# The norms' factors with tokens on the partitions: one-column sums, a power on GpSimd, a diagonal matmul

## The chip, the core and the metric

The kernel runs on one core of a Trainium2 chip. The core has TensorE (PE, matmuls; PEld is its loading of weights), VectorE (DVE), ScalarE (ACT), GpSimd (POOL) and SyncE (SP, which issues the DMAs). Each engine works through its own queue in order and waits on semaphores for the others. The metric is the device time of one execution in microseconds (us); lower is better.

## The reference, cut to what matters

A trunk of two layers over 512 tokens with 1024 features, all float32. Each layer is a half-step SwiGLU FFN, a mixer and another half-step FFN; the first layer's mixer is RWKV-7 beside an RG-LRU, the second's is stick-breaking attention. Every one of the six sub-layers has a norm ahead of it and one behind it:

```python
def rmsnorm(x, g):
    xf = x.astype(jnp.float32)
    y = xf * lax.rsqrt(jnp.mean(xf * xf, axis=-1, keepdims=True) + NORM_EPS)
    return (y * g.astype(jnp.float32)).astype(x.dtype)
...
    x = x + FFN_HALF * rmsnorm(swiglu(rmsnorm(x, ffn1_pre_g), ffn1_w_in, ffn1_w_out), ffn1_post_g)
    x = x + rmsnorm(mixer(rmsnorm(x, mix_pre_g)), mix_post_g)
    x = x + FFN_HALF * rmsnorm(swiglu(rmsnorm(x, ffn2_pre_g), ffn2_w_in, ffn2_w_out), ffn2_post_g)
```

RWKV-7 also has a group norm over each head's 64 features, `(y - mean) * lax.rsqrt(var + GN_EPS)`.

## The kernel before

Features lie on the partitions and tokens along the row: x is eight tiles of 128 features x 512 tokens. A weight comes by DMA in chunks of 128x1024 (`wraw`) and is split into a rounded part (`whi`, ScalarE) and the rest (`wlo`, VectorE); the activations are split in the same way, and each product is three matmuls (`mm3`). A sub-layer has *units* (products with the normed input) and *out tiles* (products that give its output y). Around a border between two sub-layers the work runs in halves of 256 tokens, so that the last out tiles of one half cover the norm of the other half and the first units of the next sub-layer.

A norm's factor is 1/sqrt(mean + eps) per token. The squares of the eight tiles (ScalarE) are added into one tile `acc` (GpSimd, `sumsq`); then `rsqrt` sums over the partitions. Before the change it multiplies with a matrix of ones, which leaves the sum of each token on all 128 partitions (128x256 for a half), takes the root of all of it on ScalarE and the reciprocal of all of it on VectorE. `pre` does so ahead of a sub-layer: the factor goes to `rstd`, and the units' products are multiplied with it when they leave their bank of PSUM; the tiles hi and lo of x*g that the units read don't need it. `post` does so behind a sub-layer: y * g * factor on VectorE, added to x on GpSimd (`add`), from which hi (ScalarE) and lo (VectorE, `low`) of the next sub-layer follow. That makes 23 calls of `rsqrt`, one for each half of each norm but the very last, which `last` does through `rsqrt_bank`: there the sum has tokens on the partitions already. `unit_v` of the attention takes the same factor for v with tokens on the partitions (128x4), and `chain` of RWKV-7 the group norms' factors (128x8, four times).

The order of the work is not written out. Every piece is a thread (a generator), and `Run` merges their steps by a rough clock of the engines: a step goes out when its engine would be free by the planner's costs (`cost`), by priority among equals. Behind that stands the scheduler of the tile framework, to which `emit` gives the count of the instruction as its priority, shifted for some threads by `OFFS` (`norm`, the thread of a norm ahead of a sub-layer, comes 100 later). So a change of a step's engine or cost may move other work too. A tile stands on one of 8 banks of PSUM; units may hold six of them in an FFN (`LIMIT`), three in the mixers.

All of a thread's instructions are recorded through one line of `emit`, L366 in the profile, so groups are told apart by tiles: `ones` is the matrix of ones, `eps` the added constant, `b` any tile of the arena in SBUF.

## Time and profile before

| | us |
|---|---|
| median of 3 runs | 2136.75 |
| lowest, highest | 2135.71, 2138.49 |
| the profiled execution: its span, from the first to the last instruction | 2139.7 |
| PE busy | 2060.2 |
| VectorE busy | 1229.3 |
| ScalarE busy | 863.9 |
| GpSimd busy | 488.5 |

The profile has the profiled execution's time as its span alone. Busy time is the union of an engine's instructions; matmuls are pipelined, so a PE that is busy need not be at its peak. A row of a timeline gives start, duration, engine, line, operation, output <- input, shape and count; in brackets stands how long the engine had nothing to do before it, and whose result ended that.

### The profile page before, as it was taken

How to read it: one execution, taken by the hardware profiler on the slowest of the kernel's cores; microseconds unless marked ns; L12 is line 12 of the kernel's file. 1: busy time of each engine (PE TensorE's matmuls, PEld its weight loads, DVE VectorE, ACT ScalarE, POOL GpSimd, SP SyncE). 2: the span in 40 equal slices, each digit the busy share in tenths (PEclk: the TensorE clock that was granted, in tenths of full speed). 3: DMA queues.
4: the chain of work that ended last, by engine and by line, in shares of the span. 5: the costliest groups of instructions: out<-in, count | busy, mean ns of one | idle time of the engine just before them, and what ended most of it. 6: DMA issues, size and time to landing. Idle time of an engine off the chain costs nothing. (4 is left out here: it accounts for less than half of the span.)

```text
span 2139.7 us, 29740 instructions
## 1 busy us (share of the span) xinstructions
PE 2060.2 (96%) x11916; PEld 1747.1 (82%) x11916; DVE 1229.3 (57%) x1770; ACT 863.9 (40%) x1370; POOL 488.5 (23%) x480
## 2 busy tenths in 40 slices
PE   8999999899999899999999999999999899999998
PEld 7888889877677887888898888888878789788887
DVE  6344344887786853444466354446899977344443
ACT  6322223555655443222335322233666755322221
POOL 3000013512331620100153010015232354010013
PEclk9999999999999999999999999999999999999999
DMA  5322321322113223223312322231111223333311
GB/s 195 120 93 99 101 96 51 117 58 62 35 52 104 84 82 116 88 99 108 99 60 81 117 92 98 96 99 36 54 56 60 79 80 108 99 98 99 108 51 40
DMA packets 72378, 185.54 MB, mean 87 GB/s; under 512 B 19632, under 2 KB 26928, under 8 KB 72240
## 3 DMA queue, kind: packets, MB, share of 16 engines
q1 hardware_dynamic: 72240, 183.65, 26.7%
q8 instruction: 93, 1.52, 0.3%
q14 instruction: 45, 0.37, 0.1%
HBM read 177.85 MB, written 5.77 MB: 86 GB/s over the span
## 5 line engine op out<-in xcount | busy, mean ns | idle before, releaser
L366 PE MATMUL bank<-b,b 128*128 128x512 f32 (+6 forms) x7350 | 1232.1, 330 | 28.4 <-DVE b L366 19.5
L366 PEld LDWEIGHTS bank<-b,b 128*128 128x128 f32 (+3 forms) x7350 | 1031.6, 181 | 217.8 <-DVE b L366 36.5
L366 PE MATMUL bank<-b,whi 128*128 128x512 f32 (+1 forms) x2460 | 692.4, 365 | 20.5 <-DVE b L366 10.9
L366 POOL TENSOR_TENSOR b<-b,b 128x256 f32<-128x256 f32 (+5 forms) x355 | 364.3, 1039 | 870.7 <-DVE b L366 560.6
L366 DVE TENSOR_TENSOR b<-bank,b 128x512 f32<-128x512 f32 (+7 forms) x441 | 250.6, 582 | 527.7 <-PE bank L366 520.9
L366 PEld LDWEIGHTS bank<-b,whi 128*128 128x128 f32 x2460 | 441.8, 192 | 92.6 <-DVE b L366 14.3
L366 PE MATMUL bank<-b,wlo 128*128 128x512 f32 (+1 forms) x1230 | 447.7, 364 | 0.8 <-DVE wlo L366 0.8
L366 DVE TENSOR_TENSOR b<-wraw,b 128x1024 fp32r<-128x1024 f32 (+1 forms) x194 | 267.9, 1386 | 148.7 <-ACT b L366 130.4
L366 ACT CAST b<-wraw 128x1024 fp32r<-128x1024 f32 (+1 forms) x194 | 196.6, 1024 | 333.7 <-PE bank L366 192.4
L366 PEld LDWEIGHTS bank<-b,wlo 128*128 128x128 f32 x1230 | 235.9, 192 | 34.9 <-issue 1.2
L366 POOL TENSOR_TENSOR b<-b 128x512 f32<-128x512 f32 (+5 forms) x93 | 105.5, 1144 | 683.2 <-DVE b L366 553.3
L366 ACT ACTIVATE b<-b 128x256 f32<-128x256 f32 (+1 forms) x319 | 154.3, 501 | 243.1 <-DVE b L366 204.9
L366 ACT CAST whi<-wraw 128x1024 fp32r<-128x1024 f32 (+2 forms) x143 | 144.9, 1018 | 238.5 <-PE bank L366 170.8
L366 DVE TENSOR_TENSOR wlo<-wraw,whi 128x1024 fp32r<-128x1024 f32 (+2 forms) x143 | 201.3, 1412 | 68.0 <-ACT whi L366 67.4
L366 ACT CAST b<-b 128x512 fp32r<-128x512 f32 (+3 forms) x188 | 104.8, 560 | 220.1 <-POOL b L366 185.6
L366 DVE TENSOR_TENSOR b<-b,b 128x512 fp32r<-128x512 f32 (+12 forms) x234 | 138.2, 599 | 73.5 <-ACT b L366 72.1
L366 DVE SCALAR_TENSOR_TENSOR b<-b,par,b 128x256 fp32r<-128x256 f32 (+5 forms) x209 | 151.8, 780 | 2.5 <-ACT b L366 2.2
L366 DVE TENSOR_TENSOR_SCAN b<-b,b 128x512 f32<-128x512 f32 (+1 forms) x72 | 71.5, 1019 | 7.2 <-ACT b L366 6.8
L366 ACT COPY b<-bank 128x512 f32<-128x512 f32 (+3 forms) x104 | 50.6, 500 | 61.4 <-PE bank L366 54.9
L366 ACT ACTIVATE b<-b,par 128x256 fp32r<-128x256 f32 (+1 forms) x100 | 51.2, 520 | 54.2 <-POOL b L366 47.5
L366 ACT ACT_TABLE_LOAD x49 | 62.9, 1283 | 9.5 <-PE bank L366 8.0
L366 DVE RECIPROCAL b<-b 128x256 f32<-128x256 f32 (+3 forms) x34 | 42.3, 1243 | 22.0 <-ACT b L366 21.9
(52 smaller groups left out, 623.3 us busy)
## 6 DMA issues: line engine op xcount, KB each, us to landing
wraw<-in_w_dram SPq DMA_DIRECT2D x302, 512.0 KB
wraw<-in_w_dram SPq DMA_DIRECT2D x32, 384.0 KB
b<-in_x_dram SPq DMA_DIRECT2D x16, 128.0 KB
l_mix_residual<-b SPq DMA_DIRECT2D x8, 256.0 KB
b<-l_mix_residual SPq DMA_DIRECT2D x8, 256.0 KB
out_dram<-b SPq DMA_DIRECT2D x16, 128.0 KB
rwkv_scores<-b SPq DMA_DIRECT2D x16, 64.0 KB
b<-in_aux_dram SPq DMA_DIRECT2D x2, 256.0 KB
```

Of the source, the lines that this page charges most:

```text
L366: f(*a, **k)
```

## The change

`rsqrt` now calls `rsqrt_bank`, and that no longer needs an extra tile. The sum is made per block of 128 tokens with the squares as weights and one column of ones as the moving operand, so that the tokens lie on the partitions: 128x2 for a half. A new `root` scales it and adds eps (VectorE, out of the bank), and raises it to -0.5 (GpSimd, `pow` with a constant tile `power`). VectorE multiplies the identity with each column, which gives a diagonal matrix per block; ones times this matrix spreads the factor over the partitions, in the same bank; ScalarE copies it out. `unit_v` and the group norms use `root` as well, in place of the root on ScalarE and the reciprocal. `eps` goes. The instructions are now called through a table of lambdas by the thread's name, which only gives each thread a line of its own in the profile; comments are taken out.

```diff
-        self.eps = self.cp.tile([P, 2], F32, name="eps")
-        nc.vector.memset(self.eps[:, 0:1], EPS)
-        nc.vector.memset(self.eps[:, 1:2], GN_EPS)
+        self.power = self.cp.tile([P, 8], F32, name="power")
+        nc.vector.memset(self.power, -0.5)
...
     def rsqrt(self, acc, s, out):
-        n = s.stop - s.start
-        ps = yield from self.bank()
-        self.PE.matmul(ps[:, :n], self.ones, acc[:, s], start=True, stop=True)
-        yield
-        std = yield from self.regs(n)
-        self.S.activation(std.ap, ps[:, :n], AF.Sqrt, bias=self.eps[:, 0:1], scale=1.0 / D)
+        ps = yield from self.rsqrt_bank(acc, s)
+        self.S.copy(out, ps[:, T - (s.stop - s.start) :])
         self.drop(ps)
         yield
-        self.V.reciprocal(out, std.ap)
-        self.put(std)
-        yield
-
-    def rsqrt_bank(self, acc, s, extra):
-        """the same, tokens on the partitions for the root, left in a bank"""
+
+    def root(self, out, mean, scale, eps):
+
+        self.V.tensor_scalar(out, mean, scale, eps, op0=ALU.mult, op1=ALU.add)
+        yield
+        self.G.tensor_tensor(out, out, self.power[:, : out.shape[1]], op=ALU.pow)
+        yield
+
+    def rsqrt_bank(self, acc, s, extra=None):
+
         n = s.stop - s.start
         nb = n // P
         ps = yield from self.bank()
         for b in range(nb):
-            for i, a in enumerate((acc[:, s], extra.ap)):
-                self.PE.matmul(ps[:, b : b + 1], a[:, b * P : (b + 1) * P], self.ones[:, 0:1], start=i == 0, stop=i == 1)
-        yield
-        self.put(extra)
+            parts = (acc[:, s],) if extra is None else (acc[:, s], extra.ap)
+            for i, a in enumerate(parts):
+                self.PE.matmul(ps[:, b : b + 1], a[:, b * P : (b + 1) * P], self.ones[:, 0:1], start=i == 0,
+                               stop=i == len(parts) - 1)
+        yield
+        if extra is not None:
+            self.put(extra)
         std, diag = yield from self.regs(64, n)
         c = std[:, 0:nb]
-        self.S.activation(c, ps[:, 0:nb], AF.Sqrt, bias=self.eps[:, 0:1], scale=1.0 / D)
-        yield
-        self.V.reciprocal(c, c)
-        yield
+        yield from self.root(c, ps[:, 0:nb], 1.0 / D, EPS)
         for b in range(nb):
             self.V.tensor_scalar_mul(diag[:, b * P : (b + 1) * P], self.ident, c[:, b : b + 1])
         yield
...
         V.tensor_reduce(v, c8(sq), axis=AX.X, op=ALU.add)
         yield
-        S.activation(v, v, AF.Sqrt, scale=1.0 / 64, bias=net.eps[:, 1:2])
-        yield
-        V.reciprocal(v, v)
+        yield from net.root(v, v, 1.0 / 64, GN_EPS)
...
             rc = self.rc[:, 0:4]
-            net.S.activation(rc, ps[:, 0:4], AF.Sqrt, bias=net.eps[:, 0:1], scale=1.0 / D)
+            yield from net.root(rc, ps[:, 0:4], 1.0 / D, EPS)
             net.drop(ps)
-            net.V.reciprocal(rc, rc)
```

How the order of instructions moves, at two places. In the names a number tells one tile of a pool from another (bank_85 is a tile on a bank of PSUM, b_5 holds `acc`, par the parameters with the identity); L310 is the thread `finish` (norms behind a sub-layer), L285 `norm` (norms ahead of one), L309 the main thread, L276 and L274 the evacuations.

The first place is the border from the first layer's second FFN to the second layer's first FFN, the second half's norm behind the sub-layer. PE before, the sum among the next FFN's first units:

```order
L366 MATMUL bank_87<-b_90_6053,b_81_5554 128x256
L366 MATMUL bank_87<-b_52_2434,b_25_323 128x256
L366 MATMUL bank_85<-b_5_95,ones 128x256
L366 MATMUL bank_87<-b_52_2434,b_81_5554 128x256
L366 MATMUL bank_87<-b_90_6053,b_81_5554 128x256
```

PE after:

```order
L309 MATMUL bank_84<-b_52_2433,b_83_5578 128x256
L310 MATMUL bank_85<-ones,b_5_94 128x1 x2
L309 MATMUL bank_84<-b_100_6214,b_84_5579 128x256
L309 MATMUL bank_84<-b_85_5661,b_83_5578 128x256
L309 MATMUL bank_84<-b_111_7957,b_83_5578 128x256
L309 MATMUL bank_84<-b_85_5661,b_84_5579 128x256
L309 MATMUL bank_84<-b_85_5661,b_83_5578 128x256
L309 MATMUL bank_84<-b_111_7957,b_83_5578 128x256
L309 MATMUL bank_84<-b_85_5661,b_84_5579 128x256
L309 MATMUL bank_84<-b_39_690,b_83_5578 128x256
L310 MATMUL bank_85<-b_107_7403,ones 128x256
L309 MATMUL bank_84<-b_112_7958,b_83_5578 128x256
```

Where one matmul with ones stood, two one-column sums stand now, and the spread comes eight passes of the units later.

VectorE at the same place before, with the last weight split and evacuation ahead of the norm:

```order
L366 TENSOR_TENSOR b_101_6255<-bank_89,b_101_6255 128x256
L366 TENSOR_TENSOR b_82_5555<-wraw_76,b_91_6073 128x1024
L366 TENSOR_TENSOR b_21_221<-wraw_74,b_82_5555 128x1024
L366 RECIPROCAL b_101_6255<-b_101_6255 128x256
L366 SCALAR_TENSOR_TENSOR b_108_7870<-b_99_6226,par,b_101_6255 128x256
```

VectorE after:

```order
L276 TENSOR_TENSOR b_103_6306<-bank_88,b_103_6306 128x256
L280 TENSOR_TENSOR b_24_327<-wraw_73,b_84_5579 128x1024
L310 TENSOR_SCALAR b_107_7403<-bank_85 128x2
L310 TENSOR_SCALAR b_107_7403<-par,b_107_7403 128x128 x2
L310 SCALAR_TENSOR_TENSOR b_107_7403<-b_102_6305,par,b_107_7403 128x256
```

The reciprocal has become the affine step and the two diagonal products, which stand next to each other; between them lies GpSimd's power.

The second place is the start of the attention, the first half's norm ahead of it, on PE. Before, with the sum between the units' first products of the second half:

```order
L366 MATMUL bank_85<-b_127_10323,b_21_221 128x256
L366 MATMUL bank_84<-b_119_9695,whi_79 128x256
L366 MATMUL bank_84<-b_127_10323,whi_79 128x256
L366 MATMUL bank_86<-b_5_95,ones 128x256
L366 MATMUL bank_84<-b_119_9695,wlo_80 128x256
```

After:

```order
L309 MATMUL bank_87<-b_132_10387,b_24_327 128x256
L285 MATMUL bank_82<-ones,b_5_94 128x1 x2
L309 MATMUL bank_83<-ones,b_5_94 128x1 x2
L285 MATMUL bank_82<-b_70_4174,ones 128x256
L309 MATMUL bank_89<-b_97_6153,whi_76 128x256
```

Sum and spread stand ahead of the second half's units, with only the first two sums of `unit_v` between them.

## Rows read from the trace of the kernel before

**Rows 1.** The page's head: span, then each engine's busy us, share, instructions.

```profile
span 2139.7 us, 29740 instructions
...
PE 2060.2 (96%) x11916; PEld 1747.1 (82%) x11916; DVE 1229.3 (57%) x1770; ACT 863.9 (40%) x1370; POOL 488.5 (23%) x480
```

**Rows 2.** PE's timeline: start us, us, instruction, count [idle before <-releaser].

```profile
373.43 7.00 PE L366 MATMUL bank<-b,b 128*128 128x256 f32 x57
399.18 0.58 PE L366 MATMUL bank<-b,b 128*128 128x256 f32 x1 [3.37 <-DVE b L366]
...
713.60 1.22 PE L366 MATMUL bank<-b,ones 128*128 128x256 f32 x2 [4.21 <-POOL b L366]
...
756.02 0.80 PE L366 MATMUL bank<-b,whi 128*128 128x256 f32 x2 [3.36 <-DVE b L366]
...
1115.99 1.22 PE L366 MATMUL bank<-b,ones 128*128 128x256 f32 x2 [3.99 <-POOL b L366]
...
1494.34 0.39 PE L366 MATMUL bank<-b,whi 128*128 128x256 f32 x1 [3.03 <-DVE b L366]
...
1801.82 4.38 PE L366 MATMUL bank<-b,b 128*128 128x512 f32 x18 [1.02 <-ACT b L366]
```

**Rows 3.** Groups of one shape: count | busy us, mean ns | idle before, releasers.

```profile
L366 ACT ACT_TABLE_LOAD x49 | 62.9, 1283 | 9.5 <-PE bank L366 8.0 <-PEq L2016 0.7
L366 DVE RECIPROCAL b<-b 128x256 f32<-128x256 f32 x23 | 40.2, 1748 | 17.0 <-ACT b L366 16.9
L366 DVE TENSOR_SCALAR b<-bank 128x8 f32<-128x8 f32 x4 | 0.7, 162 | 1.4 <-PE bank L366 1.4
L366 POOL TENSOR_TENSOR b<-b,b 128x127 f32<-128x127 f32 x7 | 4.5, 640 | 5.4 <-ACT b L366 3.7 <-DVE b L366 1.7
L366 POOL TENSOR_TENSOR b<-b,b 128x512 f32<-128x512 f32 x76 | 110.3, 1454 | 632.2 <-DVE b L366 493.0 <-ACT b L366 137.1 <-DMA wraw<-in_w_dram 1.2
L366 ACT COPY b<-bank 128x256 f32<-128x256 f32 x24 | 8.1, 372 | 20.3 <-PE bank L366 19.1 <-POOL b L366 1.2
```

**Rows 4.** Timelines of PE, VectorE, ScalarE at three norms behind sub-layers.

```profile
387.80 0.59 PE L366 MATMUL bank<-b,ones 128*128 128x256 f32 x2
392.14 10.23 DVE L366 SCALAR_TENSOR_TENSOR b<-b,par,b 128x256 f32<-128x256 f32 x16
...
731.32 1.05 PE L366 MATMUL bank<-b,ones 128*128 128x256 f32 x2
737.53 0.47 ACT L366 ACTIVATE b<-bank,eps 128x256 f32<-128x256 f32 x1 [4.18 <-POOL b L366]
739.89 12.21 DVE L366 SCALAR_TENSOR_TENSOR b<-b,par,b 128x256 f32<-128x256 f32 x16
...
1484.26 0.70 PE L366 MATMUL bank<-b,ones 128*128 128x256 f32 x2 [0.67 <-POOL b L366]
1487.29 5.26 DVE L366 SCALAR_TENSOR_TENSOR b<-b,par,b 128x256 f32<-128x256 f32 x7
```

**Rows 5.** Timeline of one-column sums: the factor for v, and the last norm.

```profile
1509.64 0.50 PE L366 MATMUL bank<-ones,b 128*128 128x1 f32 x4
...
2128.26 0.83 PE L366 MATMUL bank<-ones,b 128*128 128x1 f32 x6 [0.91 <-ACT b L366]
2129.19 0.26 ACT L366 ACTIVATE b<-bank,eps 128x2 f32<-128x2 f32 x1 [0.98 <-PE bank L366]
...
2129.68 0.48 DVE L366 TENSOR_SCALAR b<-par,b 128x128 f32<-128x128 f32 x2
...
2130.31 1.19 PE L366 MATMUL bank<-b,ones 128*128 128x256 f32 x2 [1.22 <-DVE b L366]
```

**Rows 6.** GpSimd's timeline ahead of the wait at 1115.99.

```profile
1104.55 11.39 POOL L366 TENSOR_TENSOR b<-b,b 128x256 f32<-128x256 f32 x9 [0.58 <-ACT b L366]
```

**Rows 7.** ScalarE's timeline ahead of the wait at 1801.82.

```profile
1800.00 1.28 ACT L366 ACT_TABLE_LOAD   x1
1801.29 0.47 ACT L366 ACTIVATE b<-bank,eps 128x256 f32<-128x256 f32 x1
```

43 lines of the change are left out of this document (42 added, 1 removed).

## The prediction

> **What bounds the kernel now.** I read the page's head first [rows 1]: TensorE (PE) is busy 2060 of 2139.7 us, so all that can be won without touching its matmuls is some 80 us of its idle time, and anything that makes PE issue more has to be hidden in those 80 us. ScalarE, VectorE and GpSimd are busy 40, 57 and 23% of the span; they matter only where PE waits for them. So I next took PE's own timeline and looked for rows with a bracket, its waits [rows 2]. The long ones beside the norms stand at the borders of the six sub-layers: 3.37 us at 399.18 (first FFN to first mixer), 4.21 at 713.60 and 3.36 at 756.02 (mixer to FFN), 3.99 at 1115.99 (FFN to FFN), 3.03 at 1494.34 (FFN to attention), 1.02 at 1801.82 (attention to FFN). Between the borders, inside an FFN, PE does not wait. The reader is to see who releases these waits: VectorE or GpSimd five times, ScalarE once. The rest of the idle time lies in the two mixers, at the first loads and behind the last matmul, where a norm has little part.
>
> **What the change takes away.** 23 norms (12 ahead of sub-layers, 11 behind) lose a 128x256 square root on ScalarE and a 128x256 reciprocal on VectorE of 1.75 us [rows 3]; four group norms and the one root for v lose small ones. Of the 49 table loads [rows 3] the order of instructions after has 29 left: 20 x 1.28 = 25.7 us of ScalarE. What these cost on a path is read from three norms behind sub-layers, from the sum's first pass on PE to VectorE's first product with the factor [rows 4]: 387.80 to 392.14 = 4.34 us, 731.32 to 739.89 = 8.57, 1484.26 to 1487.29 = 3.03.
>
> **What it adds on PE.** The sum with 256 columns was two passes; now two blocks of one column each, in two passes, make four, and the spreading matmul with 128x256 is again two passes. So PE issues four passes more per norm. Four one-column passes took 0.50 us [rows 5], so 0.5 x 23 = 11.5 us. They cannot be free: PE is full on both sides of most norms.
>
> **What it adds as a wait.** The sum and the spread are now two visits to PE, and between them lie VectorE, GpSimd, VectorE. PE works its queue in order, so when it comes to the spread too early, all that stands behind it, the next units' products, waits too. The last norm of the kernel before already has this form, with a root on ScalarE [rows 5]: the last one-column pass ends at 2128.26 + 0.83 = 2129.09, ScalarE starts 0.10 later, the two diagonal products take 0.48 and the spread starts 0.15 after them. For the new chain I put 0.10 + 0.16 (affine of 8 columns from a bank [rows 3]) + 0.10 (hop) + P + 0.10 (hop) + 0.48 + 0.15 = 1.09 + P, where P is GpSimd's power of two columns. No row has a power. GpSimd's nearest rows are 0.64 us for 128x127 and 1.45 us for 128x512 [rows 3]; a line through both gives about 0.4 for two columns, the power itself may cost more than a product. I take P = 0.7, near the narrowest row, and keep 0.4 to 1.45. So 1.8 us, bounds 1.5 and 2.5.
>
> What covers it are the passes that the order puts between the two visits. A pass takes (7.00 - 0.28) / 56 = 0.12 us [rows 2]. Counting them in the order for the 23 norms gives 0.48 us once (the first norm of attention), 0.96 three times, 1.3 to 1.8 eleven times, and 2.2 to 6.5 for the rest. Adding up what is missing to the chain gives 5.5 us at 1.8, 2.9 at 1.5 and 16.8 at 2.5. While the power runs VectorE stands too: in 21 of 24 norms the diagonal products are the very next thing in its queue, so what is queued there (weight splits, the products with the factor, evacuations) waits 0.1 + P + 0.1 = 0.9 us. VectorE's work per norm goes from 1.75 to 0.16 + 0.48 = 0.64, so 0.2 us is what it keeps of the 1.1 it saved. GpSimd gets 0.7 us more per norm; the power stands right behind the last addition to the sum or among the residual additions.
>
> The Trainium skill (SBUF — State Buffer, "SBUF: two separate sides") says that VectorE instructions with two inputs in SBUF and GpSimd instructions that read SBUF exclude each other on a shared port. The trace agrees as far as it goes: nine additions took 11.39 us, 1.27 each, while VectorE split weights [rows 6], against 0.64 for the narrower row. By that rule a power would wait for a running VectorE instruction; but VectorE mostly stands waiting for the power, and only where something lies between would the sum grow, by my estimate of under 3 us in all.
>
> **How much of PE's cost is hidden.** Norm by norm, by the waits of [rows 2]: at 399.18 the wait follows the second half's norm behind the sub-layer, which is hidden. At 756.02 it follows that norm and the first norm ahead, two hidden. At 1115.99 GpSimd sets the end, having run without a break from 1104.55 to 1115.94 [rows 6], so the first half's norm behind the sub-layer is hidden. At 1494.34 two more. That makes 6; the other 17 stand before a chain's start or behind the last wait of their border. So 17 x 0.5 = 8.5 us and 5.5 x 17 / 23 = 4.1 us of stalls fall on the path.
>
> **What the chains give back.** From the sum to the first product with the factor the new way takes 0.6 (four passes and their end) + 1.8 + 0.6 (spread) + 0.5 (ScalarE's copy of 0.37 [rows 3] with its hops) = 3.5 us. Against 4.34 that is 0.8 us won at 399.18. Against 8.57, up to the whole wait of 3.36 at 756.02; the long part there is the root, which ScalarE started only at 737.53, with GpSimd named as what it waited for [rows 4]. The new way has no root on ScalarE, but it visits GpSimd and ScalarE as well, so the gain could also be nothing; I take 3.4. Against 3.03 it loses 0.5 at 1494.34. At 1801.82 PE waits 1.02 us for a weight's cast on ScalarE, which had a table load of 1.28 and a root in its queue from 1800.00 on [rows 7]; that goes: 1.0. At the very end 2129.09 to 2129.68 = 0.59 becomes 0.10 + 0.16 + 0.10 + 0.7 + 0.10 = 1.16, so 0.6 more. Other relief from 25.7 us less on ScalarE is between nothing and 5 us (five waits like the one at 1801.82); I take 2.5.
>
> The Trainium skill (ScalarE: Activation LUTs, "What ACT_TABLE_LOAD costs") counts a drain of 1.38 us to each load, 2.66 in all. The trace does not: the load at 1800.00 ends at 1801.28 and the root starts at 1801.29 [rows 7]. By the page the relief would be about twice as large and the sum 2.5 us lower.
>
> **The sum.** +8.5 + 4.1 - 0.8 - 3.4 + 0.5 - 1.0 + 0.6 - 2.5 = +6.0 us. The profile gives its execution by the span alone, 2139.7 us, 2.9 above the median of 2136.75; I carry the difference over to the median: 2142.8.
>
> **Rivals.** (a) *Hidden or balanced.* PE's added passes are swallowed by waits that exist, because a border's end is set by GpSimd's additions (as at 1115.99, and they are not made shorter). With half as many norms on the path (6.3 instead of 12.6) the sum is -0.3: 2136.5. For it: GpSimd and VectorE release five of six waits. Against it: PE has no wait after the second norm ahead at most borders.
> (b) *Faster.* The other side. The place is PE's two waits for GpSimd, 4.21 at 713.60 and 3.99 at 1115.99, where the planner put the sum's matmul ahead of its operand. The planner books the new steps with other lengths, and if at both places the sum comes late enough, 8.2 us go; the stalls on the path shrink with P near 0.4 by 2.6 x 17 / 23 = 1.9; and the two passes of the sum behind each of these waits took 1.22 us against 0.59 at 387.80 [rows 2, 4], 0.6 each. That gives 6.0 - 8.2 - 1.9 - 1.2 = -5.3: 2131.4. It decides from the point where the sum's first pass comes after GpSimd's last addition. Against it: at 1115.99 the order after puts the sum 166 rows behind the one before it, 163 before, so PE comes there no later.
> (c) *The power is long.* At P = 1.45 the stalls on the path are 16.8 x 17 / 23 = 12.4 instead of 4.1, the chains take 0.75 more at three places, 2.2, and give back nothing at 756.02: 6.0 + 8.3 + 2.2 + 3.4 = +19.9: 2156.7.
> (d) *The order itself.* The planner is greedy, and the mixers' instructions come in another order after as well. Nothing in the profile prices this; it is why the range reaches 4 us beyond the sums at the lower end.
>
> **How the numbers follow.** My forecast is +6.0, 2142.8; its own range from P and the shares is 2138 to 2149. About 0.2% (4.3 us) is what a measurement of this kernel can tell from no change. Chances: forecast 0.43, of which 0.08 ends within 0.2%; (a) 0.22, all within; (b) 0.27; (c) 0.08. So faster 0.27, same 0.08 + 0.22 = 0.30, slower 0.35 + 0.08 = 0.43. The range: (b) less the 4 us of (d), rounded, to (c): 2128 to 2157.
>
> **What would show it.** Right: 29 table loads; PE's instructions up by 4 passes in each of 23 norms; PE rows of the spread with waits of 0.2 to 1.5 us released by VectorE; powers of 0.4 to 1.0 us; waits at the borders about as long as before. Wrong: powers over 1.5 us; the waits at 713.60 and 1115.99 gone; spreads without waits; or a difference that lies inside a mixer, away from all norms.

## The result, and the profile after

The changed kernel takes 2205.75 us (median of 4 runs), the kernel before 2137.62 us beside it: a ratio of 1.0313, 95% interval 1.0297 to 1.033. It is slower by 68 us where 6 were forecast, and far outside the range.

The page's head after, its answer to [rows 1], and the granted clock in 40 slices:

```profile
span 2204.2 us, 29945 instructions
...
PE 2099.5 (95%) x12008; PEld 1776.7 (81%) x12008; DVE 1202.1 (55%) x1815; ACT 833.0 (38%) x1344; POOL 507.2 (23%) x509
...
PEclk9999999998998899999999999999999999999999
```

PE has 92 passes more, which is 4 for each of 23 norms, as counted. But it is busy 39 us more, not 11.5. Some of its passes must run slower, and the eights in the clock's line, in slices 10, 13 and 14 (about 496 to 551 and 661 to 772 us), say where: in the first mixer and just behind it. It is so in every run: over the whole the granted clock is 0.970 to 0.972 in the four runs of the changed kernel, and 0.982 to 0.987 in the runs of the kernel before that were timed beside the experiments.

**Where the 64.5 us of span arise.** I cut both executions at the norms' sums, which have a tile of their own (`ones`). A border runs from the first pass of the first half's sum behind a sub-layer to the first pass of the second half's sum ahead of the next; a sub-layer from there to its own first sum. For mixer 0 these are the two rows here, first of the kernel before (its end is the wait at 713.60 in [rows 2]), then of the changed one (start us, us, instruction, count):

```profile
413.75 0.59 PE L366 MATMUL bank<-b,ones 128*128 128x256 f32 x2
```

```profile
427.70 0.50 PE L285 MATMUL bank<-ones,b 128*128 128x1 f32 x4
...
757.98 1.01 PE L310 MATMUL bank<-ones,b 128*128 128x1 f32 x4 [4.04 <-POOL b L277]
```

So mixer 0 took 713.60 - 413.75 = 299.9 us before and 757.98 - 427.70 = 330.3 after. All stages in the same way: start to the first border +3.2, border into mixer 0 +10.8, **mixer 0 +30.4**, the other four borders +13.8, the three later FFNs +6.3, mixer 1 -1.1, the end +1.1. That is 64.5. Nearly half of the loss lies in a stage whose changed instructions are four group norms and, at its start, the end of the norm that opens it (the spread at 430.65).

**What happens in mixer 0.** A stage's length is PE's idle time, plus its busy time times the granted clock (work at full clock), plus the rest of its busy time (what the lower clock costs). Mixer 0 before: 12.9 idle + 278.3 work + 8.6 lower clock. After: 26.4 + 273.5 + 30.4. So the work did not grow beyond what such a split can tell (the clock has two digits, which is 1.5 us each); 13.5 us are idleness and some 20 us lower clock. The last 100 us of the mixer show both. Busy time of all engines of the changed kernel (columns: stretch, its length, busy us of PE, PEld, DVE, ACT, POOL with counts, granted clock, DMA share, GB/s):

```profile
660.00:680.00 20.00, 19.73 (x177) 14.40 (x177) 18.86 (x39) 12.47 (x22) 3.39 (x3) 1.00 0.36 100
680.00:700.00 20.00, 8.52 (x136) 7.58 (x134) 14.13 (x17) 14.30 (x18) 10.11 (x7) 0.66 0.39 125
700.00:720.00 20.00, 20.00 (x172) 14.12 (x172) 2.10 (x5) 2.80 (x7) 0.53 (x1) 1.00 0.04 14
720.00:740.00 20.00, 14.76 (x140) 12.37 (x140) 6.50 (x15) 2.61 (x6) 3.72 (x3) 0.74 0.30 93
```

The same stretches, counting only instructions that touch the rounded weights `whi`, the large products of the units and out tiles (PE, PEld, DVE, ACT, then the clock):

```profile
680.00:700.00 20.00, 0.15 (x1) 0.16 (x1) 0.00 (x0) 0.00 (x0) 0.66 0.39 125
700.00:720.00 20.00, 7.92 (x24) 4.12 (x24) 0.00 (x0) 0.00 (x0) 1.00 0.04 14
720.00:740.00 20.00, 0.00 (x0) 0.00 (x0) 0.00 (x0) 0.00 (x0) 0.74 0.30 93
```

Two rows of PE's timeline after, the longest wait of the first of these stretches, and in the last one large products whose weights are no `whi` (out tiles of a half, 128x256):

```profile
687.74 2.06 PE L291 MATMUL bank<-b,b 64*64 64x64 f32 x32 [4.21 <-DVE b L280]
...
733.60 3.94 PE L309 MATMUL bank<-b,b 128*128 128x256 f32 x31
```

And in the kernel before, 47 us earlier, about equally far from the mixer's end:

```profile
633.00:653.00 20.00, 6.64 (x18) 3.22 (x18) 1.21 (x1) 2.09 (x2) 1.00 0.20 58
653.00:673.00 20.00, 7.96 (x24) 4.35 (x24) 1.21 (x1) 0.00 (x0) 1.00 0.33 106
673.00:693.00 20.00, 6.46 (x19) 3.38 (x18) 0.00 (x0) 0.00 (x0) 1.00 0.46 145
```

The mixer has two kinds of work for PE: the recurrence of four pairs of heads, chains of small matmuls that wait for VectorE and ScalarE at every step, and the large products, which wait for little and fill what the chains leave open. Before, 5 to 8 us of products with `whi` stand in every 20 us from 593 to 693. After, they come in lumps. From 680 to 700 one of them is left: PE runs the small products of a pair almost alone (L291 is the thread `inverse`), idles 11.5 us, and its clock falls to 0.66. From 720 to 740 there is none, and the 37 half-row products stand together from 733.60 on, behind 13 us of the pair's chain alone. That the lumps cause the loss is read from such stretches; no run moves the large products by themselves. The clock falls without idleness too. In 5 us pieces of the changed kernel around 530 us:

```profile
520.00:525.00 5.00, 5.00 (x32) 4.14 (x31) 4.42 (x15) 3.22 (x5) 0.53 (x1) 1.00 0.29 105
525.00:530.00 5.00, 5.00 (x48) 3.69 (x48) 4.45 (x14) 2.63 (x4) 1.20 (x1) 0.78 0.00 0
530.00:535.00 5.00, 5.00 (x28) 3.60 (x27) 0.00 (x0) 0.11 (x1) 0.07 (x1) 0.50 0.10 26
535.00:540.00 5.00, 5.00 (x28) 3.74 (x28) 1.36 (x4) 1.36 (x3) 0.00 (x0) 0.50 0.01 3
```

From 525 to 535 no pass touches a `whi`: PE issues only the pairs' products with 64 or 128 columns, is busy without a gap, and its clock falls to half (1.2 in place of 2.4 GHz), in which it stays until some time after 545; large products return from 535 on.

**What happens at the norms.** PE's waits by line over the whole span, after (L310 is the thread of the norms behind sub-layers, L285 of those ahead; total, times, longest):

```profile
PE bank L310 <- DVE b L310: 11.5, 5, 3.8
PE bank L285 <- DVE b L285: 11.2, 6, 4.7
...
PE bank L309 <- DVE b L284: 6.9, 14, 1.8
...
PE bank L310 <- POOL b L276: 5.3, 3, 3.0
PE bank L310 <- POOL b L277: 4.5, 2, 4.0
```

The first two are the waits at the spread: 22.7 us, of which 1.62 are the last norm's, where PE waited 1.22 before too [rows 5]; in the 23 changed halves it is 21.1. Waits for GpSimd at the sums stayed, 4.04 us at 757.98 for the 4.21 at 713.60 and 2.96 at 1160.32 for the 3.99 at 1115.99 [rows 2]. The last norm shows the chain with all engines free (PE, VectorE, GpSimd):

```profile
2192.39 0.83 PE L310 MATMUL bank<-ones,b 128*128 128x1 f32 x6 [0.91 <-ACT b L276]
2193.33 0.16 DVE L310 TENSOR_SCALAR b<-bank 128x2 f32<-128x2 f32 x1 [1.50 <-PE bank L310]
2193.57 0.71 POOL L310 TENSOR_TENSOR b<-b,power 128x2 f32<-128x2 f32 x1 [3.30 <-DVE b L310]
2194.31 0.48 DVE L310 TENSOR_SCALAR b<-par,b 128x128 f32<-128x128 f32 x2 [0.82 <-POOL b L310]
...
2194.84 1.22 PE L310 MATMUL bank<-b,ones 128*128 128x256 f32 x2 [1.62 <-DVE b L310]
```

1.62 us from the end of the sum to the spread. The second half's norm at the border into mixer 0 is the same work with VectorE's queue in the way (VectorE's row ahead of it first, from its own timeline):

```profile
394.52 0.69 DVE L298 TENSOR_TENSOR b<-b,b 128x512 fp32r<-128x512 f32 x1 [1.80 <-ACT b L298]
...
391.15 0.61 PE L310 MATMUL bank<-ones,b 128*128 128x1 f32 x4 [1.62 <-POOL b L276]
395.13 0.15 DVE L310 TENSOR_SCALAR b<-bank 128x2 f32<-128x2 f32 x1
395.36 0.71 POOL L310 TENSOR_TENSOR b<-b,power 128x2 f32<-128x2 f32 x1 [4.26 <-DVE b L310]
396.10 0.48 DVE L310 TENSOR_SCALAR b<-par,b 128x128 f32<-128x128 f32 x2 [0.82 <-POOL b L310]
...
396.64 1.22 PE L310 MATMUL bank<-b,ones 128*128 128x256 f32 x2 [3.83 <-DVE b L310]
```

The sum ends at 391.76, but the affine of two columns starts at 395.13: VectorE stood behind a split of the mixer's own weights (L298) that waited for ScalarE. From the sum's end to the affine it is 0.03 to 0.33 us in 14 of the 24 norms, 1.0 to 4.3 us in the other 10, 26 us in all.

These waits are not all new idle time. PE is idle 2139.7 - 2060.2 = 79.5 us before and 2204.2 - 2099.5 = 104.7 after; without the mixer's 12.9 and 26.4 that is 66.6 and 78.3, 11.7 us more. The waits at sums and spreads grew by 20.9 us (14.8 in all before, 35.7 after). The difference is in waits that went: 3.37 us at 399.18, 3.36 at 756.02 and 3.03 at 1494.34 [rows 2] were waits for VectorE behind the norms, at other products. After, no wait in the borders is longer than 1.93 us but those at sums and spreads: PE stands at the spread in place of a later product.

### The profile page after: what moved, and what is told of

It reads as the page before. It is cut to its first block, busy times and chain, and to the rows that moved or that the text cites. A ratio compares the mean times of both kernels' runs of the same rounds, so it can differ in the third digit from the quotient of the medians.

```text
span 2204.2 us, 29945 instructions
## 1 busy us (share of the span) xinstructions
PE 2099.5 (95%) x12008; PEld 1776.7 (81%) x12008; DVE 1202.1 (55%) x1815; ACT 833.0 (38%) x1344; POOL 507.2 (23%) x509
## 4 chain that ended last, share of the span: by engine, by line
PE 75%; DVE 11%; POOL 4%; ACT 3%; issue 2%; DMA 1%; DVEq 0%; POOLq 0%; SPq 0%; ACTq 0%
PE bank L309 67%; DVE b L302 3%; PE bank L291 2%; PE bank L292 2%; DVE b L310 2%; POOL b L285 2%; DVE b L284 1%; PE bank L302 1%; DVE b L274 1%; PE bank L290 1%; DVE b L280 1%; DVE wlo L280 1%; DMA wraw<-in_w_dram 1%; PE bank L310 1%; POOL b L292 1%
## 5 line engine op out<-in xcount | busy, mean ns | idle before, releaser
L309 PE MATMUL bank<-b,b 128*128 128x512 f32 (+1 forms) x5437 | 1065.7, 354 | 10.6 <-DVE b L284 5.7
L309 PEld LDWEIGHTS bank<-b,b 128*128 128x128 f32 x5437 | 901.2, 191 | 152.1 <-DVE b L284 8.5
L309 PE MATMUL bank<-b,whi 128*128 128x512 f32 (+1 forms) x2444 | 696.0, 368 | 13.3 <-ACT b L283 8.2
L309 PEld LDWEIGHTS bank<-b,whi 128*128 128x128 f32 x2444 | 443.4, 194 | 85.8 <-ACT b L283 8.9
L309 PE MATMUL bank<-b,wlo 128*128 128x512 f32 (+1 forms) x1222 | 448.4, 367 | 0.8 <-DVE wlo L280 0.8
L274 DVE TENSOR_TENSOR b<-bank,b 128x512 f32<-128x512 f32 (+1 forms) x237 | 143.3, 618 | 320.1 <-PE bank L309 311.5
L309 PEld LDWEIGHTS bank<-b,wlo 128*128 128x128 f32 x1222 | 236.7, 194 | 35.6 <-issue 1.5
L274 POOL TENSOR_TENSOR b<-b 128x512 f32<-128x512 f32 (+1 forms) x58 | 66.9, 1156 | 582.7 <-DVE b L274 493.3
L274 POOL TENSOR_TENSOR b<-b,b 128x512 f32<-128x512 f32 (+1 forms) x42 | 54.4, 1295 | 481.9 <-DVE b L274 441.3
L274 ACT CAST b<-b 128x512 fp32r<-128x512 f32 (+3 forms) x160 | 88.6, 556 | 200.8 <-POOL b L274 181.1
L276 DVE TENSOR_TENSOR b<-bank,b 128x256 f32<-128x256 f32 (+1 forms) x88 | 47.6, 543 | 173.9 <-PE bank L309 173.9
L274 DVE TENSOR_TENSOR b<-b,b 128x512 fp32r<-128x512 f32 (+3 forms) x140 | 91.5, 654 | 62.6 <-ACT b L274 61.6
L274 ACT ACTIVATE b<-b 128x512 f32<-128x512 f32 (+1 forms) x100 | 57.1, 576 | 99.1 <-DVE b L274 98.9
L285 POOL TENSOR_TENSOR b<-b,b 128x256 f32<-128x256 f32 x84 | 83.0, 988 | 36.4 <-ACT b L285 32.5
L287 POOL TENSOR_TENSOR b<-b,b 128x256 f32<-128x256 f32 x88 | 76.7, 901 | 23.8 <-DVE b L310 23.4
L310 DVE SCALAR_TENSOR_TENSOR b<-b,par,b 128x256 f32<-128x256 f32 x87 | 65.3, 810 | 11.5 <-ACT b L310 9.7
L276 POOL TENSOR_TENSOR b<-b,b 128x256 f32<-128x256 f32 (+1 forms) x51 | 44.8, 879 | 95.8 <-ACT b L276 95.1
L284 DVE SCALAR_TENSOR_TENSOR b<-b,par,b 128x256 fp32r<-128x256 f32 x96 | 63.8, 711 | 2.3 <-ACT b L283 2.2
```

The lines of the kernel that those rows point to most:

```text
L274: "unit_ev": lambda f, a, k: f(*a, **k),
L276: "third_ev": lambda f, a, k: f(*a, **k),
L284: "low": lambda f, a, k: f(*a, **k),
L285: "norm": lambda f, a, k: f(*a, **k),
L287: "add": lambda f, a, k: f(*a, **k),
L309: "main": lambda f, a, k: f(*a, **k),
```

## The experiments

Two questions: is mixer 0's loss the power (in the group norms, or through the late border ahead), or the order that the planner made of the instructions? And what do the norms themselves cost? `LAG[1]` is a number of the planner: how many planned us the thread that ends a sub-layer's second half holds back. "Plan" is the length of mixer 0 by the planner's own rough clock, which the expectations quote. In the table it runs from the first pair's first matmul to the first sum behind the mixer. The first four expectations count the border ahead as part of the mixer, in the plan and on the chip (there 350.9 us before, 392.1 changed). Figures of a stage come from one profiled execution each, and with a clock of two digits the split of a mixer's length is good to 1.5 us; the length itself was 9 us apart in two executions of one order (the last experiment). Since the cut follows PE's order, it can also move work between a border and the stage behind it. Outside is the span less mixer 0, against the 1839.8 us of before.

| kernel | ratio to before [95%] | plan of mixer 0 | mixer 0, us | idle + lower clock there | outside, us |
|---|---|---|---|---|---|
| before | 1 | 269.8 | 299.9 | 12.9 + 8.6 | 0 |
| changed | 1.0313 [1.0297, 1.033] | 293.9 | 330.3 | 26.4 + 30.4 | +34.1 |
| norm_old | 1.0011 [0.9995, 1.0027] | 268.9 | 303.0 | 18.3 + 8.5 | +0.1 |
| b_lag4 | 1.0128 [1.0101, 1.0154] | 305.6 | 336.6 | 27.8 + 27.8 | -4.4 |
| b_lag0 | 1.0084 [1.0066, 1.0103] | 270.3 | 304.4 | 12.8 + 11.7 | +12.0 |
| a_lag2 | 1.0224 [1.0193, 1.0256] | 263.9 | 308.9 | 16.0 + 11.7 | +36.1 |
| late2 | 1.0168 [1.013, 1.0205] | 271.8 | 306.4 | 16.1 + 8.7 | +23.2 |
| cost_real | 1.0239 [1.0207, 1.0271] | 278.3 | 323.2 | 15.9 + 21.5 | +25.1 |
| gn_old | 1.0321 [1.0292, 1.035] | 304.9 | 335.3 | 26.7 + 27.8 | +31.9 |
| pre_new | 1.0283 [1.0263, 1.0302] | 294.4 | 337.8 | 27.2 + 24.8 | +23.6 |
| post_new | 1.0178 [1.016, 1.0196] | 257.9 | 313.0 | 10.2 + 24.2 | +24.2 |
| mult_for_pow | 1.0257 [1.0236, 1.0277] | 293.9 | 322.3 | 22.7 + 24.0 | +31.7 |
| gn_mult | 1.0278 [1.0256, 1.03] | 293.9 | 325.3 | 23.7 + 24.1 | +35.4 |
| norm_old_lag1 | 1.0143 [1.0117, 1.0168] | 273.9 | 320.0 | 19.8 + 15.0 | +5.2 |
| lag1_gn_mult | 1.0111 [1.0088, 1.0133] | 273.9 | 328.7 | 16.7 + 31.2 | +4.7 |

### norm_old: the two-half norms undone

```diff
     def rsqrt(self, acc, s, out):
-        ps = yield from self.rsqrt_bank(acc, s)
-        self.S.copy(out, ps[:, T - (s.stop - s.start) :])
+        n = s.stop - s.start
+        ps = yield from self.bank()
+        self.PE.matmul(ps[:, :n], self.ones, acc[:, s], start=True, stop=True)
...
+        self.V.reciprocal(out, std.ap)
```

> The changed kernel with the 22 two-half norms (pre and post) of the old form again: 128x128 sum, root on ScalarE, reciprocal on VectorE. The group norms of the RWKV mixer, the factor for v and the last norm stay with the power on GpSimd. Theory A (the order of instructions in mixer 0 is what costs some 30 us; the power itself is cheap there): the planner's own length for mixer 0, from the first sum of the post norm ahead of it to the first sum of its own post norm, is 316.2 us for this kernel, against 317.0 for the kernel before and 338.0 for the changed one, so mixer 0 should take on the chip the 350.9 us of before within 6 us, not the 392.1 of after, and the whole kernel 2130 to 2142 us. Theory B (the power of the group norms, queued on GpSimd, delays the mixer): mixer 0 stays 25 us or more over before, the whole kernel at 2160 to 2175 us.

Measured: 2145.67 us against 2143.64, no difference (both a little above the range of theory A), mixer 0 at 303.0, with the border ahead 354.0, within 6 of 350.9 as theory A had it. The power in the group norms, in v's factor and in the last norm costs nothing that can be measured in this order. So the whole loss hangs on the norms ahead of and behind the sub-layers, though nearly half of it appears in a stage that has none inside but the end of one.

### b_lag4: the old instructions, another order

```diff
-LAG = (0.0, 3.0, 0.0)
+LAG = (0.0, 4.0, 0.0)
```

> Every instruction of the kernel before (no norm is touched), with the same number of the planner moved the other way: the lag ahead of the second half's post norm is 4 us in place of 3. Its own length for mixer 0 is then 354.7 us, against 317.0 for the kernel before. Theory A (order): mixer 0 takes 380 to 410 us on the chip in place of 350.9, with none of the changed norms in it, and the whole kernel 2165 to 2200 us. Theory B (the power and the norms' new form cost the mixer its time): a lag of one microsecond at five places moves the whole by no more than 6 us, 2132 to 2143 us.

Measured: 2169.36 us, mixer 0 at 336.6, +36.7, without one changed norm. (The expectation counts the border ahead as part of the mixer: 336.6 + 54.2 = 390.8, inside its 380 to 410.) It has the same signature as the changed kernel, +14.9 us idle and +19.2 lower clock, and the same stretch, 80 us from the mixer's end:

```profile
673.00:693.00 20.00, 10.36 (x65) 6.93 (x64) 16.42 (x19) 16.66 (x23) 10.00 (x7) 0.79 0.52 151
```

An order alone is enough for the whole of mixer 0's loss.

### a_lag2 and cost_real: the changed instructions, other orders

The first sets `LAG[1]` to 2. The second tells the planner what the power takes:

```diff
+        if k.get("op") == ALU.pow:
+            return 0.39 + 0.157 * n, 0.15
         return 0.1 + (1.1e-3 if op in self.FAST else 2.25e-3) * n, 0.15
```

> Every instruction of the changed kernel, but one number of the planner is moved: the lag ahead of the second half's post norm is 2 us in place of 3. The planner then writes mixer 0 out in another order; its own length for the mixer is 306.0 us (338.0 for the changed kernel, 317.0 for the kernel before). Theory A (order): mixer 0 takes on the chip 340 to 355 us, against 392.1 in the changed kernel, and the whole kernel comes to 2150 to 2175 us; what is left over the kernel before is the borders' share of some 20 to 25 us, since the chain with the spread is unchanged there. Theory B (the power itself): mixer 0 stays at 380 us or more and the whole at 2195 to 2210 us.

> The changed kernel, with the planner told what the power takes: 0.39 us and 0.157 us for each column (0.71 us for two columns, 1.02 for four, 1.65 for eight), where it reckoned 0.10 to 0.12 us. The instructions are those of the changed kernel; the spread stands later in TensorE's queue and mixer 0 comes in another order (the planner's own length 323.3 us, 338.0 for the changed kernel). Theory A: mixer 0 at 350 to 370 us. For the borders: if the waits of TensorE at the spreads come from a power that is longer than planned, they go from 22.7 us to under 10 us and the borders give back 10 us or more, the whole at 2140 to 2165 us; if the waits come from VectorE and ScalarE being late at the borders whatever the power takes, they stay at 18 us or more and the whole is 2160 to 2180 us. Theory B (the power holds GpSimd up in mixer 0): the mixer stays over 380 us and the whole over 2185 us.

Measured, a_lag2: 2188.79 us. Counted from its own start the mixer falls from 330.3 to 308.9, with every power in place; with the border it is 367.1, because the border stayed 7.2 us long and the mixer 9 over before. That lies between the 340 to 355 of theory A and the 380 of theory B, and so does the whole. What lies outside mixer 0 did not gain (+36.1). An order that changes no instruction gives back 21 us of the mixer, less than theory A's plan said.

Measured, cost_real: 2191.67 us, above what theory A allowed and in theory B's range. The mixer fell by 7 only, though its plan was 15 shorter; with the border it is 379.8, 10 over theory A's range and next to theory B's 380. By its own expectation this run speaks for theory B; gn_old and gn_mult below decide against it. The waits at the spreads went from 22.7 to 11.8 us (7.0 and 4.8 in the two threads), and what lies outside mixer 0 from +34.1 to +25.1: 9 us for 11 us of waits. In the borders themselves nothing shows, 284.9 us for 285.4; the gain is in the FFNs behind them, 955.5 for 964.2, as it would be if PE did their first units where it had waited. PE's idle time outside the mixer fell by 5.4 us (78.3 to 72.9), not by 11: the waits for VectorE at the next sub-layer's operands (L284) rose from 6.9 to 12.8.

### gn_old: the group norms undone

```diff
...
-        yield from net.root(v, v, 1.0 / 64, GN_EPS)
+        S.activation(v, v, AF.Sqrt, scale=1.0 / 64, bias=net.eps[:, 1:2])
+        yield
+        V.reciprocal(v, v)
```

> The changed kernel with only the group norms of the RWKV mixer undone: the root on ScalarE and the reciprocal on VectorE again, no power in mixer 0's own chains. The planner's own length for mixer 0, from the first pair's first matmul to the first sum of the post norm, is 304.9 us for it, against 293.9 for the changed kernel and 269.8 for the kernel before. On the chip, mixer 0 from the last sum of the pre norm to the first sum of its post norm took 330.3 us in the changed kernel and 299.9 in the kernel before. Theory A (order): undoing this part makes the mixer no faster but as slow or slower, 328 to 348 us, the whole kernel 2200 to 2225 us. Theory B (the power on GpSimd holds the mixer up): mixer 0 returns to 300 to 310 us and the whole to 2175 to 2185 us.

Measured: 2209.14 us, mixer 0 at 335.3, 5 us more than with the power, less than two executions of one order can differ by (9 us, the last experiment). Taking the power out of the mixer's own chains does not help. Theory B, that the power on GpSimd holds the mixer up, falls.

### pre_new and post_new: one kind of norm at a time

```diff
# pre_new, in post:
-        yield from self.rsqrt(self.acc, s, rs.ap)
+        yield from self.rsqrt_old(self.acc, s, rs.ap)
# post_new, in pre:
-            yield from self.rsqrt(self.acc, s, self.rstd[:, s])
+            yield from self.rsqrt_old(self.acc, s, self.rstd[:, s])
```

> The changed kernel with the post norms of the old form and the pre norms, the group norms, v's factor and the last norm of the new one. Planner's own length of mixer 0: 294.4 us (before 269.8, changed 293.9). Theory A (order for the mixer, the new form of the norms for the borders): mixer 0 at 322 to 338 us; the five borders together, from the first half's post sum to the second half's pre sum, lie 8 to 16 us over the 260.8 us of before, where the changed kernel has 285.4; the whole 2175 to 2200 us. Theory B (the mixer's loss comes from the slow borders ahead of it): half of the border's loss leaves half of the mixer's, mixer 0 at 310 to 318 us, the whole 2160 to 2175 us.

> The changed kernel with the pre norms of the old form and the post norms, the group norms, v's factor and the last norm of the new one. Planner's own length of mixer 0: 257.9 us, the shortest of all (before 269.8, changed 293.9). Theory A: mixer 0 at 288 to 303 us, no longer than the 299.9 of before, with the group norms' power in it; the five borders 8 to 16 us over the 260.8 us of before; the whole 2140 to 2165 us. Theory B (the mixer's loss comes from the slow borders ahead of it): mixer 0 at 310 to 318 us, the whole 2160 to 2175 us.

Measured: pre_new 2201.67 us, mixer 0 at 337.8 and borders +13.4 us, as theory A had it (the whole 2 us above its range). post_new is a miss: with the shortest plan of all, mixer 0 took 313.0, not 288 to 303, the borders are 27.4 us longer, not 8 to 16, and the whole, 2179.45, is above both theories' ranges. PE idled less there than in the kernel before (10.2); it lost 24.2 to the lower clock. So the plan's length orders kernels only roughly: the kernels with plans near 270 lie at 300 to 306, those with plans over 290 at 322 to 338, but 257.9 gave 313.0, 263.9 gave 308.9, 278.3 gave 323.2 and (below) 273.9 gave 320.0. The planner reckons with a lower clock of PE too, by a rule of its own (`warm`); no run here tests how near that comes to what the chip grants. Theory B here, a late border that pushes the mixer, would also fit the 313.0. pre_new has the slowest mixer of all and a border into mixer 0 that is 4.6 us *shorter* than before by this cut, but that decides nothing: its sum stands early there, and the first 64x512 product of a pair, 65.4 us after the first half's sum, comes some 6 us later than before (58.9). Two other runs exclude theory B: late2 (below) has a border 8.5 us longer than before and a mixer of 306.4, and norm_old_lag1 a border 1.7 us shorter and a mixer of 320.0. Nor do the two halves of the change add up, at the borders (13.4 + 27.4 against 24.6 for both) or outside mixer 0 (23.6 + 24.2 against 34.1).

### late2: the spread put later

```diff
             self.V.tensor_scalar_mul(diag[:, b * P : (b + 1) * P], self.ident, c[:, b : b + 1])
         yield
+        if extra is None:
+            yield Ev(self.run.new.t + 2.0)
```

> The changed kernel with the spread's matmul put off by 2 planned us in each of the 22 two-half norms, so that more of TensorE's other work stands ahead of it. Planner's own length of mixer 0: 271.8 us. Theory S (at the borders TensorE's waits at the spread, and the lower clock behind them, are what is lost beyond the added passes): the waits at the spreads go from 22.7 us to under 6 us, and all that lies outside mixer 0 comes from 35 us over before to 15 to 22 us over; with mixer 0 at 300 to 315 us the whole is 2155 to 2175 us. Theory C (the norm's factor is what is late, whoever waits for it): the waits go away and as much comes back at the evacuations and the banks behind them; outside mixer 0 it stays 30 us or more over before, the whole 2170 to 2190 us.

Measured: 2174.95 us, the fastest kernel with all norms new; mixer 0 at 306.4. The waits at the spreads went from 22.7 to 10.6 us, not under 6, and outside mixer 0 it is +23.2, between the two theories. PE's waits for VectorE at the next sub-layer's operands (the thread `low`, L284), 6.9 us in the changed kernel, say where the waits went:

```profile
PE bank L309 <- DVE b L284: 21.4, 19, 4.2
```

12.1 us left the spreads and 14.5 came back there, as theory C had it: the factor is late, whoever waits for it. PE's idle time outside the mixer fell by 1.5 us only (2169.4 - 2076.5 - 16.1 = 76.8 for 78.3). So the 10.9 us won outside the mixer are busy time, not the waits; no run isolates them.

### mult_for_pow and gn_mult: the power taken out, the order held

```diff
-        nc.vector.memset(self.power, -0.5)
+        nc.vector.memset(self.power, 1.0)
...
-        self.V.tensor_scalar(out, mean, scale, eps, op0=ALU.mult, op1=ALU.add)
+        self.V.tensor_scalar(out, mean, scale, 0.25, op0=ALU.mult, op1=ALU.min)
...
-        self.G.tensor_tensor(out, out, self.power[:, : out.shape[1]], op=ALU.pow)
+        self.G.tensor_tensor(out, out, self.power[:, : out.shape[1]], op=ALU.mult)
```

This is mult_for_pow; gn_mult does the like in the four group norms alone, where GpSimd multiplies the bounded mean by itself. Both leave the root out.

> The changed kernel with the power taken out and nothing moved: GpSimd multiplies by ones where it raised to the power -0.5, and the VectorE instruction ahead of it bounds the mean by 0.25 in place of adding epsilon, so the root is left out and the numbers stay finite. Every engine's instructions stand in the same order, row for row, as in the changed kernel. Theory A (the order costs mixer 0 its time, the power costs only its own length): mixer 0 keeps 322 to 332 us (330.3 in the changed kernel, 299.9 in the kernel before); at the norms the chain is some 0.5 us shorter, so the waits of TensorE at the spreads go from 22.7 us to 12 to 18 us and the whole kernel to 2188 to 2203 us. Theory B (the power itself, in the group norms or ahead of the mixer): mixer 0 falls to 300 to 312 us, the whole to 2165 to 2180 us.

> The changed kernel with the power taken out of the four group norms of mixer 0 alone: GpSimd multiplies the bounded mean by itself there, so that root is left out. The order of the instructions is that of the changed kernel on every engine; the 25 other powers stay. In the run with all powers replaced mixer 0 fell from 330.3 to 322.3 us. If those 8.0 us are the group norms' power (1.65 to 2.48 us each, on the path of each pair's chain): mixer 0 at 321 to 325 us and the whole 2194 to 2199 us. If they come from the norms at the mixer's ends and from how the stage happens to start: mixer 0 at 328 to 333 us and the whole 2200 to 2207 us. In neither case does it come near the 299.9 us of before, which the order theory forbids as long as the order stays.

Groups of GpSimd's instructions with the constant tile (ns: least, median, largest), the changed kernel, then mult_for_pow:

```profile
L285 POOL TENSOR_TENSOR b<-b,power x12: 696/708/882, 25.1 to 1855.3; 128x2 f32<-128x2 f32 x12
L310 POOL TENSOR_TENSOR b<-b,power x12: 707/707/708, 366.6 to 2193.6; 128x2 f32<-128x2 f32 x12
L292 POOL TENSOR_TENSOR b<-b,power x4: 1644/1649/2483, 574.9 to 736.4; 128x8 f32<-128x8 f32 x4
L309 POOL TENSOR_TENSOR b<-b,power x1: 1018/1018/1018, 1568.1 to 1568.1; 128x4 f32<-128x4 f32 x1
```

```profile
L310 POOL TENSOR_TENSOR b<-b,power x12: 194/194/195, 370.1 to 2183.6; 128x2 f32<-128x2 f32 x12
L292 POOL TENSOR_TENSOR b<-b,power x4: 203/204/1043, 571.2 to 733.3; 128x8 f32<-128x8 f32 x4
```

Measured: with every power shortened by 0.5 us (two columns) or 1.4 us (eight), the order the same row for row, the kernel takes 2195.3 us, 10.5 less, or 13 less when each is counted against the kernel before beside it (2140.17 and 2137.62). With the group norms' powers alone shortened it takes 2203.3, 2.5 less, or 8 counted so (2143.58), and its interval overlaps that of the changed kernel. Mixer 0 goes to 322.3, as theory A had it, and to 325.3, between the two ranges of its expectation. So some 10 to 13 of the 68 us are the power's own length, and in this order most of mixer 0's loss stands without any power. The waits at the spreads fell from 22.7 to 15.5 us only: two thirds of them are not the power. And this is the one run that shortens them in a fixed order: for 7.2 us of waits what lies outside mixer 0 got 2.4 us shorter (+31.7 for +34.1), though PE's idle time there fell by 5.8 (78.3 to 72.5).

### b_lag0: a search for a faster order

> Every instruction of the kernel before, the planner's lag ahead of the second half's post norm at 0 us in place of 3. Planner's own length of mixer 0 270.3 us (269.8 before), its own end 18 us earlier than that of before (1949.7 against 1967.8). If the planner's times carry over to the chip: mixer 0 at 296 to 306 us, the five borders 5 to 15 us shorter than the 260.8 of before, the whole 2122 to 2135 us, faster than both kernels. If the lag covers sums that really come late (TensorE waits for GpSimd's squares at five first sums of before): the borders don't shorten, 2138 to 2155 us.

Measured: 2158.5 us, above the second range too. `LAG[1]` at 0 (the edit is that of b_lag4 with another number) made the planner's own end 18 us earlier and the chip slower by 0.84%. Its mixer kept its length, 304.4, as planned. The waits of PE at the sums went from 14.8 to 31.1 us: the lag covers sums that really come late. No kernel of this study beats the one before.

### norm_old_lag1 and lag1_gn_mult: a case against the order theory

norm_old with `LAG[1]` at 1, then the same with the group norms' power replaced as in gn_mult.

> The changed kernel with the two-half norms of the old form (power in the group norms, in v's factor and in the last norm) and the same lag at 1 us. Planner's own length of mixer 0 273.9 us, its own end 1959.5 us (1967.8 for the kernel before, 1963.9 with a lag of 3). Order theory: mixer 0 at 300 to 312 us with the group norms' power in it, the whole 2132 to 2150 us. If the power in the mixer costs by itself, hidden so far by a lucky order: mixer 0 over 315 us and the whole over 2155 us.

> The kernel with two-half norms of the old form and a lag of 1 us, the power taken out of its four group norms in the same way, nothing moved. With the power its mixer 0 took 320.0 us, more than the order theory allowed, so the power in the group norms was left as a suspect. Order theory: the mixer's excess over 299.9 us stays for the most part, 312 to 320 us, the whole 2158 to 2169 us. Power theory: mixer 0 falls to 300 to 306 us and the whole to 2145 to 2152 us.

Measured: norm_old_lag1 2169.43 us, mixer 0 at 320.0, which by its expectation speaks for the power. lag1_gn_mult settles it: without the power the same order takes 2167.93 us, 1.5 less (5 counted against the kernel before beside it, the intervals overlapping), and in its profiled execution (2175.21, the longest of its four runs) mixer 0 took 328.7, more than either theory's range. The group norms' power is not the cause of this mixer's excess. The pair also shows how far one profile can be trusted for this stage: with the same order on every engine the two readings lie 9 us apart, in the lower clock (15.0 and 31.2), not in idle time (19.8 and 16.7).

## Why the prediction was wrong

**The step that failed first: rival (d), the order.** The prediction saw that the planner writes the mixers out in another order, found that nothing in the profile prices it, and gave it 4 us at the lower end of the range alone. It was the largest term. Mixer 0 lost 30.4 us; other orders of the same changed instructions gave back 21 to 24 of them (a_lag2, late2) or 7 (cost_real), and an order of the old instructions lost 36.7 (b_lag4). The kernel before had a sign of it: PE is busy 287 of 300 us in this mixer, with large products between the chains nearly throughout, so there is much to lose when they come in lumps. How much, no row says. The sentence on what would make the prediction wrong, "a difference that lies inside a mixer, away from all norms", is what happened for nearly half of the loss.

**The power: right, by luck.** P was put at 0.7 and measured 0.71, but no row had a power, and the line through the products that stood behind it gives 0.4 us at two columns where a product takes 0.19 (mult_for_pow). The chain of 1.8 us is 1.62 when the engines are free. Of the under 3 us that the prediction allowed for powers that wait for a running VectorE instruction, little shows: 22 of the 24 two-column powers took 0.70 to 0.71 us, two 0.88.

**The stalls at the spread: 21.1 us in the 23 halves, forecast 5.5 gross and 4.1 on the path.** The failed step is the hop of 0.10 us from the bank to the affine. The affine stands in VectorE's in-order queue, and at 10 of 24 norms it came 1.0 to 4.3 us late; three powers waited 1.4 to 3.0 us more in GpSimd's. The passes that the planner put between sum and spread did not cover this; told the power's true length it still left 11.8 of the 22.7 us (cost_real). What a us of these waits costs the kernel is not settled: outside mixer 0 cost_real won 9.0 us for 10.9, late2 10.9 for 12.1 with the waits back at another place, mult_for_pow 2.4 for 7.2. The old form went through ScalarE and VectorE too, and there PE waited at later products, 3.37, 3.36 and 3.03 us [rows 2]; with a second visit it waits earlier. Net of that PE's idle time outside the mixer grew by 11.7 us, still well over the 4.1.

**The added passes: their number right, their cost not pinned.** 92 passes, by the prediction's 0.5 us for a norm 11.5 us. Of the 34.1 us outside mixer 0, 11.7 are idle time and 22.4 busy time. The lower clock takes 6 to 7 of these (the clock of the whole is 0.984 before and 0.971 after; less the mixer's share), so some 16 are work at full clock, where the passes were to bring 11.5. (To add the passes to the growth of the waits at sums and spreads, 20.9 us, would give 32.4 of the 34.1, but it leaves out the waits that went.) In post_new, with 11 new norms only and +24.2, PE waits 10.5 us behind its start for the casts of the next sub-layer's operands (L283), where the changed kernel has 3.7. What the rest is was not isolated.

**What the chains were to give back: next to nothing came.** From the sum to the first product, 4.34 us was to become 3.5 and became 398.36 - 391.15 = 7.2; 8.57 was to lose up to 3.36 and became 785.07 - 776.43 = 8.6; 3.03 was to become 3.5 and became 1539.96 - 1536.54 = 3.4. The first two have the late VectorE in them. Of 49 table loads 29 were left, as counted, and one wait went with them: the 1.02 us at 1801.82 have no counterpart, PE's products run on without a wait from 1856.93 to 1881.53. That term, 1.0, was right; it is made up for by a wait of 1.13 at the spread just ahead. The other 2.5 us do not show. By the Trainium skill (ScalarE: Activation LUTs, "What ACT_TABLE_LOAD costs") the loads would have been worth twice the engine time; no gain of either size appears.

**Rivals (a), (b) and (c).** (a) fell with the borders. (b) was right to be doubted: both waits for GpSimd stayed. (c) gave a price near the stalls' true size (16.8 against 21.1) for a wrong reason, a long power.

**What stays open.** Why the chip takes 28 to 55 us more than the plan for this mixer (most in post_new) and why one order's mixer can differ by 9 us between executions: the 9 us lie in the granted clock, and so does most of what post_new's mixer took more than that of before (24.2 us of lower clock against 8.6, with less idleness). No run here holds the order and moves the clock alone. The lumps are not all of it either. In 10 us pieces from the mixer's start, those with less than 2.5 us of products with 256 or 512 columns number 3 before and hold 3.7 us of idleness and lower clock; in the changed kernel they are 7 with 25.4, in b_lag4 7 with 26.2; but norm_old_lag1 has 3 with 4.7, and its loss is in the other pieces. And no run takes the 34 us outside the mixer apart in full.

## What to carry to other kernels

When instructions are placed by a greedy planner, a small edit re-rolls the order of every stage behind it: measure the same edit in several orders, and hold the order row for row (a cheaper operation in the same place) to price an operation by itself. A step that sends PE's result through other engines and back to PE is priced by the queues of those engines, not by the durations and hops of a free chain; read what stands ahead in VectorE's queue at each place. A wait that goes at one place can come back at the next, so count PE's whole idle time, not the waits of one kind. Filler work is a resource: count in every 20 us stretch how much of it is left before trusting that a stage is bound by PE.

## What the runs showed of the hardware

GpSimd's power of float32 took 0.71 us for 128x2, 1.02 for 128x4 and 1.65 for 128x8, about 0.39 + 0.157 us for each column, whereas a product of the same shapes took 0.19 and 0.20. Eight columns of it cost more than a product of 512 columns (1.45 us, [rows 3]).

TensorE's clock was granted at half, 0.50 in each 5 us piece from 530 to 545 us, while the engine was busy without a gap; ahead of it, from 525 on, stood only products with 64 or 128 columns. A full PE row on the page is no sign of full speed.
